# Weight sums of the four-quarter products formed on GpSimd, and the norms' scales loaded through ScalarE's queue

## Chip, core and metric

The kernel runs on one core of a Trainium2 chip. The metric is the device time of one execution in microseconds; lower is better. Three executions of the kernel before took 1226.11, 1226.34 and 1227.87 us.

## What is computed

The reference is one layer of a decoder trunk over 512 tokens of width 1024: a SwiGLU feed-forward network (FFN), a mixer (sparse attention, a short convolution and gates), attention over a memory, and a second FFN. Each stands between two RMS norms and is added to the running sum. The change lies in the two FFNs and in the load of the norms' scales:

```python
def rms_norm(x, g):
    xf = x.astype(jnp.float32)
    y = xf * lax.rsqrt(jnp.mean(xf * xf, axis=-1, keepdims=True) + EPS)
    return (y * g.astype(jnp.float32)).astype(x.dtype)
def swiglu(x, w1, w3, w2):
    return (jax.nn.silu(x @ w1) * (x @ w3)) @ w2
f = swiglu(rms_norm(h, ffn1_pre_g[l]), ffn1_w1[l], ffn1_w3[l], ffn1_w2[l])
h = h + 0.5 * rms_norm(f, ffn1_post_g[l])
```

The inner width of an FFN is 2816, that is 22 column blocks of 128.

## The kernel before

**Precision.** Every float32 operand of a product is split into a high part that TensorE takes (fp32r) and the remainder, and a product is three matmuls: high by high, high by low, low by high. `Weights.split` does it for weights: ScalarE casts the loaded tile `wraw` to `wh`, VectorE subtracts to `wl` (for a half tile both lie in one tile `whl`).

**Four-quarter products.** Most of the column blocks of `w1` and `w3` are not multiplied plainly. `ffn` takes two neighbouring blocks of one of the two matrices and `quad` forms their product with all 512 tokens by seven products of quarters instead of eight: the inner dimension of 1024 is cut in two, the two blocks are the other cut, and the tokens are cut in two halves. The text calls such a product a quad. There are 16 in FFN 1 and 18 in FFN 2; each pair of them (first `w1`, then `w3`) makes two blocks of the FFN's inner activations, and products with `w2` stand between. In `quad` each of the seven products is 12 matmuls of 128x256. They use, in this order, the weight factors "raw" (the upper block's two quarters, two products), "sums" (two products), "more" (two) and "last" (one). With the upper block's quarters T0, T1 and the lower block's L0, L1:

- sums: L0 + L1 and L0 + T0
- more: L0 + L1 + T0 and L0 + L1 + T0 + T1
- last: L1

**How the factors are made before.** `Weights.__init__` lists groups (one raw tile of 128x1024 each) and jobs (one split each). For a quad the group of sums loads L0 twice through SyncE's queue (SP), and `load` then issues two further transfers on GpSimd's queue (POOL) that add L1 and T0 to what lies in the tile while they move (`accum_op`, L126). When the job "sums" has been split, VectorE turns the same tile into "more" by two additions of 128x512 (L161, L162), and it is split again. The L1 quarters of a pair share one further tile. A pair takes five raw tiles.

**What sets the order.** `fetch` splits ahead of use, up to eight half tiles (`PIECES_AHEAD`), and each split calls `load` for the groups up to six tiles further (`RAW`, the raw tiles that there are). A scheduler then fixes the order of instructions on each engine when the program is built; each engine runs its own list in order, so an instruction that waits holds up all behind it. Loads signal through eight semaphores in turn, so a load on the hardware queues can be held until the load eight places earlier has landed. After the second quad of a pair VectorE multiplies the two results (`o<-o`), ScalarE casts the product (`hidh`, L321), and the weights of the next quads follow behind that cast in ScalarE's list.

**The start.** The scales of all norms (`gains`, 36 KB) are loaded once through POOL's queue (L293). ScalarE's queue carries two of the first weight tiles, SP's the rest and x. The first operand that TensorE needs is u = x times gain, made by `split_scaled` (L325 on ScalarE, then VectorE), and the first split weights `whl`.

Of the kernel before, what the change touches and what calls it, by code (L numbers as in the profile page):

```python
# [12 lines left out]
ALU = mybir.AluOpType  # L13
# [18 lines left out]
UNIT = 1024  # L32
PIECE = 512
# [40 lines left out]
class Weights:  # L74
# [6 lines left out]
    def __init__(self, tc, raw_pool, pool, items):  # L81
        self.nc, self.raw_pool, self.pool = tc.nc, raw_pool, pool
        self.items, self.groups, self.jobs, self.where = items, [], [], []
        room = 0
        for n, item in enumerate(items):
            src = item[0]
            if item[1] == "quad":
                self.where.append((len(self.jobs), 0))
                i, g = item[2], len(self.groups)
                top, low = src[0], src[1]  # L90
                self.groups.append([(top, 0, UNIT)])
                self.groups.append([(low[:, :PIECE], o, PIECE) for o in (0, PIECE)]
                                   + [(low[:, PIECE:], 0, 0), (top[:, :PIECE], PIECE, 0)])
                if i == 0:
                    last = g + 2
                    self.groups.append([(low[:, PIECE:], 0, PIECE), (item[3][1][:, PIECE:], PIECE, PIECE)])
                self.jobs += [(g, "raw", None), (g + 1, "sums", None), (g + 1, "more", None), (last, i, None)]
                room = 0
                continue
            w = src.shape[1]  # L100
            fresh = room < w
            if fresh:
                self.groups.append([])
                room = UNIT
            o = UNIT - room
            self.groups[-1].append((src, o, w))
            g = len(self.groups) - 1
            if n < FIRST:
                self.where.append((len(self.jobs), 0))
                self.jobs.append((g, o, o + w))  # L110
            elif fresh or o + w - self.jobs[-1][1] > UNIT:
                self.where.append((len(self.jobs), 0))
                self.jobs.append((g, o, o + w))
            else:
                self.where.append((len(self.jobs) - 1, o - self.jobs[-1][1]))
                self.jobs[-1] = (g, self.jobs[-1][1], o + w)
            room -= w
        self.raw, self.ready, self.held = {}, {}, {}
        self.nd = self.np = self.ni = 0

    def load(self, upto):
        while self.nd < min(upto, len(self.groups)):
            t = self.raw_pool.tile([P, UNIT], F32, tag="wraw", name="wraw", bufs=RAW)
            for src, o, w in self.groups[self.nd]:
                if w == 0:
                    self.nc.gpsimd.dma_start(t[:, o:o + PIECE], src, accum_op=ALU.add)  # L126
                    continue
                queue = self.nc.scalar if self.nd < 2 and o == 0 else self.nc.sync
                queue.dma_start(t[:, o:o + w], src)
            self.raw[self.nd] = t  # L130
            self.nd += 1

    def slots(self, j):
        _, c, end = self.jobs[j]
        return (2 if isinstance(c, str) else 1) if end is None else -(-(end - c) // PIECE)

    def split(self, src):
        shape = list(src.shape)
# [12 lines left out]
    def prepare(self, j):  # L151
        g, c, end = self.jobs[j]
        self.load(g + RAW)
        if end is not None:
            return self.split(self.raw[g][:, c:end])
        t = self.raw[g]
        if c in (0, 1):
            return self.split(t[:, c * PIECE:(c + 1) * PIECE])
        if c == "more":
            top, v = self.raw[g - 1], self.nc.vector  # L160
            v.tensor_add(t[:, :PIECE], t[:, :PIECE], top[:, :PIECE])  # L161
            v.tensor_add(t[:, PIECE:], t[:, :PIECE], top[:, PIECE:])  # L162
        return self.split(t.rearrange("p (j k) -> p j k", j=2))

    def ahead(self, upto):
        while self.np < min(upto, len(self.jobs)):
# [52 lines left out]
def build(tc, a, out):  # L219
    nc = tc.nc  # L220
    vec, ten = InOrder(tc, nc.vector), InOrder(tc, nc.tensor)
    ctx = ExitStack()
    with ctx:
# [36 lines left out]
        order = []  # L260
        for ffn in (1, 2):
            up, down = a[f"up{ffn}"], a[f"down{ffn}"]
# [16 lines left out]
            for p in ffn_plan(ffn):  # L279
                if p == ("plain", 0) or p == ("plain", 1):  # L280
                    order += [up[p[1], :, c] for c in (0, 1)] if ffn == 2 else []
                elif p[0] == "plain":
                    order += [up[p[1], :, c] for c in (0, 1)]
                elif p[0] == "quad":
                    order.append((up[p[1]:p[1] + 2, :, p[2]], "quad", p[2], up[p[1]:p[1] + 2, :, 1]))
                elif p[2][1] == 0:
                    order += across(p[2][0], p[1])
            order += across(0, len(SLABS) - 1) + across(1, len(SLABS) - 1)
# [1 line left out]


        gains = con.tile([P, len(GAINS), KD], F32, name="gains")
        nc.gpsimd.dma_start(gains, a["gains"])  # L293
        xts = [slot([P, 2, T], F32, "x") for _ in range(KD // 2)]
        x0 = [xts[i // 2][:, i % 2] for i in range(KD)]

# [608 lines left out]
        for c in range(4):  # L905
            pg, pc = bank("pgc"), bank("pci")
            product(pg, ws.unit(), u)
            t = ev([P, T], F32, "gc")
# [6 lines left out]
            for k in (1, 0):  # L915
                o = 2 - k
# [35 lines left out]
        for f in range(KD):  # L952
            if f < GATES:
                g = ga[f]
# [243 lines left out]
```

## Time and profile before

| | |
|---|---|
| median of three runs | 1226.34 us |
| the profiled execution's own time | 1225.09 us |
| its span, first to last instruction | 1223.3 us |
| TensorE (PE) busy | 1205.3 us, 99% |
| VectorE (DVE) busy | 861.1 us, 70% |
| ScalarE (ACT) busy | 569.4 us, 47% |
| GpSimd (POOL) busy | 82.9 us, 7% |
| bytes moved | 160.93 MB |

PE stands for matmuls and PEld for the weight loads before them, which overlap them. A row of the list of waits names who waited, at which line, for whom, and then the total in us, the number of waits and the longest one. In a timeline, the bracket at a row's end is the time that the engine had been idle and what ended it.

### The profile page before, as it was taken

The numbers are of one execution on the slowest core, as the hardware profiler recorded it, in microseconds if no ns is written. First come the engines' busy times: TensorE is split into PE (matmuls) and PEld (weight loads), VectorE is DVE, ScalarE is ACT, GpSimd is POOL, SyncE is SP. The second block draws the span as 40 slices with busy tenths as digits, with TensorE's granted clock in tenths as the row PEclk, the third lists the DMA queues.
The fourth block names the chain that finished last, engine by engine and source line by source line (L and its number), as shares of the span: only waits on it lengthen the run. The fifth ranks groups of instructions, "written<-read, shape, count | busy, mean of one in ns | idle before, by whom it ended". The sixth has DMA issues, their size and how long they took to land.

```text
span 1223.3 us, 18630 instructions
## 1 busy us (share of the span) xinstructions
PE 1205.3 (99%) x7198; PEld 1073.8 (88%) x7198; DVE 861.1 (70%) x1524; ACT 569.4 (47%) x991; POOL 82.9 (7%) x123
## 2 busy tenths in 40 slices
PE   7999999999999999999999999999999999999997
PEld 7889999999889888888887898888989999999986
DVE  6877577776777799964357785464768658776665
ACT  6445343433454365455453583453844434343241
POOL 0001111101002400000000000000000011110100
PEclk9999999999999999999999999999999999999999
DMA  8335656555715632222222545223435655755641
GB/s 311 86 93 155 163 142 173 157 155 137 242 60 155 174 120 84 77 90 79 69 70 86 172 121 172 69 77 131 139 68 155 155 144 155 176 156 142 145 139 69
DMA packets 62376, 160.93 MB, mean 132 GB/s; under 512 B 7872, under 2 KB 10432, under 8 KB 62288
## 3 DMA queue, kind: packets, MB, share of 16 engines
q1 hardware_dynamic: 50752, 138.74, 35.3%
q0 software_dynamic: 11104, 20.23, 10.0%
q8 instruction: 56, 0.92, 0.3%
q10 hardware_dynamic: 432, 0.79, 0.2%
q14 instruction: 32, 0.26, 0.1%
HBM read 150.81 MB, written 4.19 MB: 127 GB/s over the span
## 4 chain that ended last, share of the span: by engine, by line
PE 86%; DVE 7%; ACT 4%; issue 1%; DMA 1%; DVEq 0%; SPq 0%; ACTq 0%; POOLq 0%
PE q L212 28%; PE pf L212 21%; PE pgb L212 4%; PE ph L212 4%; PE pga L212 4%; PE pq L212 4%; PE pa L212 3%; PE pb L212 3%; PE pkx L212 2%; PE pvx L212 2%; ACT sq L432 2%; PE pya L212 2%; DVE f L212 2%; DVE wl L146 1%; PE pyb L212 1%
## 5 line engine op out<-in xcount | busy, mean ns | idle before, releaser
L146 DVE TENSOR_TENSOR wl<-wraw,wh 128x1024 fp32r<-128x1024 f32 x248 | 296.3, 1218 | 113.1 <-ACT wh L145 100.2
L145 ACT CAST wh<-wraw 128x1024 fp32r<-128x1024 f32 x248 | 253.2, 1049 | 112.0 <-DVE wraw L162 91.7
L212 PE MATMUL q<-rt,wh 128*128 128x256 f32 x816 | 148.4, 283 | 0.0
L212 PEld LDWEIGHTS q<-rt,wh 128*128 128x128 f32 x816 | 127.3, 192 | 0.0
L126 POOL DMA_DIRECT2D wraw<-in_up x68 | 58.6, 924 | 947.3 <-DMA wraw<-in_up 705.4
L212 PE MATMUL q<-rt,wl 128*128 128x256 f32 x408 | 115.7, 283 | 0.0
L212 PE MATMUL pf<-wh,hidh 128*128 128x512 f32 (+1 forms) x278 | 107.3, 386 | 0.0
L212 PE MATMUL pf<-wl,hidh 128*128 128x512 f32 (+1 forms) x278 | 107.2, 385 | 0.0
L212 PE MATMUL pf<-wh,hidl 128*128 128x512 f32 (+1 forms) x278 | 106.9, 384 | 0.0
L212 DVE TENSOR_TENSOR o<-o,q 128x512 f32<-128x512 f32 (+1 forms) x136 | 71.8, 549 | 12.0 <-PE q L212 9.7
L212 PE MATMUL q<-u,wh 128*128 128x256 f32 x432 | 79.2, 283 | 0.0
L212 PEld LDWEIGHTS q<-rt,wl 128*128 128x128 f32 x408 | 78.3, 192 | 0.3 <-DVE wl L146 0.3
L212 PE MATMUL q<-r,wh 128*128 128x256 f32 x384 | 70.4, 283 | 0.0
L212 PEld LDWEIGHTS q<-u,wh 128*128 128x128 f32 x432 | 68.4, 192 | 1.3
L212 PEld LDWEIGHTS q<-r,wh 128*128 128x128 f32 x384 | 60.9, 192 | 1.2
L212 PEld LDWEIGHTS pf<-wh,hidl 128*128 128x128 f32 x278 | 52.3, 188 | 10.5
L212 PE MATMUL q<-u,wl 128*128 128x256 f32 x216 | 61.1, 283 | 0.0
L212 PEld LDWEIGHTS pf<-wh,hidh 128*128 128x128 f32 x278 | 52.3, 188 | 9.8
L212 PEld LDWEIGHTS pf<-wl,hidh 128*128 128x128 f32 x278 | 52.3, 188 | 9.5
L321 ACT CAST hidh<-o 128x1024 fp32r<-128x1024 f32 x17 | 17.9, 1052 | 91.9 <-DVE o L212 91.9
L212 PE MATMUL pgb<-u,wh 128*128 128x512 f32 x192 | 59.3, 389 | 0.0
L212 DVE TENSOR_TENSOR f<-f,pf 128x512 f32<-128x512 f32 (+1 forms) x49 | 33.0, 673 | 33.0 <-PE pf L212 32.7
(265 smaller groups left out, 2671.6 us busy)
## 6 DMA issues: line engine op xcount, KB each, us to landing
wraw<-in_up SPq DMA_DIRECT2D x108, 256.0 KB, 4.7
wraw<-in_up SPq DMA_DIRECT2D x50, 512.0 KB, 5.2
wraw<-in_down SPq DMA_DIRECT2D x44, 512.0 KB, 4.4
wraw<-in_w_in SPq DMA_DIRECT2D x37, 512.0 KB, 4.5
wraw<-in_up POOLq DMA_DIRECT2D x68, 256.0 KB, 5.5
wraw<-in_w_out SPq DMA_DIRECT2D x8, 512.0 KB, 3.7
wraw<-in_w_k SPq DMA_DIRECT2D x8, 512.0 KB, 4.1
wraw<-in_w_v SPq DMA_DIRECT2D x8, 512.0 KB, 4.5
```

The costliest lines, as they stand in the source:

```text
L126: self.nc.gpsimd.dma_start(t[:, o:o + PIECE], src, accum_op=ALU.add)
L145: self.nc.scalar.copy(hi, src)
L146: self.nc.vector.tensor_sub(lo, src, f32(hi))
L212: ins = f(*args, **kwargs)
L321: nc.scalar.copy(dst_h, src)
L432: ins = nc.scalar.activation(ev([P, T], F32, "sq")[:, cols], src, AF.Square, accum_out=part)
```

## The change

Each quad now has three raw tiles. Two are loaded, the upper block and the lower block, each once and whole (512 KB). The third is not loaded: two GpSimd additions fill it with "sums" (L123, L124 of the new file), and when that has been split, two more GpSimd additions turn it into "more" (L157, L158). "last" is read from the lower block's tile. The two loads of L0, the shared L1 loads, the two accumulating transfers and VectorE's two additions are gone. The load of `gains` moves from POOL's queue to ScalarE's, ahead of the two weight loads there. Lines after the edit move up by some four, so that the subtraction of `split` is L146 before and L141 now.

```diff
-                i, g = item[2], len(self.groups)
-                top, low = src[0], src[1]
-                self.groups.append([(top, 0, UNIT)])
-                self.groups.append([(low[:, :PIECE], o, PIECE) for o in (0, PIECE)]
-                                   + [(low[:, PIECE:], 0, 0), (top[:, :PIECE], PIECE, 0)])
-                if i == 0:
-                    last = g + 2
-                    self.groups.append([(low[:, PIECE:], 0, PIECE), (item[3][1][:, PIECE:], PIECE, PIECE)])
-                self.jobs += [(g, "raw", None), (g + 1, "sums", None), (g + 1, "more", None), (last, i, None)]
+                g = len(self.groups)
+                self.groups += [[(src[0], 0, UNIT)], [(src[1], 0, UNIT)], []]
+                self.jobs += [(g, "raw", None), (g + 2, "sums", None), (g + 2, "more", None), (g + 1, "last", None)]
...
             for src, o, w in self.groups[self.nd]:
-                if w == 0:
-                    self.nc.gpsimd.dma_start(t[:, o:o + PIECE], src, accum_op=ALU.add)
-                    continue
                 queue = self.nc.scalar if self.nd < 2 and o == 0 else self.nc.sync
                 queue.dma_start(t[:, o:o + w], src)
+            if not self.groups[self.nd]:
+                top, low = self.raw[self.nd - 2], self.raw[self.nd - 1]
+                self.nc.gpsimd.tensor_add(t[:, :PIECE], low[:, :PIECE], low[:, PIECE:])
+                self.nc.gpsimd.tensor_add(t[:, PIECE:], low[:, :PIECE], top[:, :PIECE])
...
-        if c in (0, 1):
-            return self.split(t[:, c * PIECE:(c + 1) * PIECE])
-        if c == "more":
-            top, v = self.raw[g - 1], self.nc.vector
-            v.tensor_add(t[:, :PIECE], t[:, :PIECE], top[:, :PIECE])
-            v.tensor_add(t[:, PIECE:], t[:, :PIECE], top[:, PIECE:])
-        return self.split(t.rearrange("p (j k) -> p j k", j=2))
+        if c == "last":
+            return self.split(t[:, PIECE:])
+        res = self.split(t.rearrange("p (j k) -> p j k", j=2))
+        if c == "sums":
+            top, add = self.raw[g - 2], self.nc.gpsimd.tensor_add
+            add(t[:, :PIECE], t[:, :PIECE], top[:, :PIECE])
+            add(t[:, PIECE:], t[:, :PIECE], top[:, PIECE:])
+        return res
...
-        nc.gpsimd.dma_start(gains, a["gains"])
+        nc.scalar.dma_start(gains, a["gains"])
```

The order in which the built program's instructions stand moves at three places that the prediction speaks of.

ScalarE at the start of the program; DMAHW0 to DMAHW7 are the eight semaphores of the hardware queues, DMASW0 is that of POOL's queue. Before:

```order
L129 DMA wraw<-in_up 128x512 x2
L307 ACT_TABLE_LOAD
L307 ACTIVATE warm<-ones 128x1 [waits DVE_49]
L349 ACTIVATE sq<-x 128x256 [waits DMAHW1_49]
L325 ACTIVATE u<-x,gains 128x256 [waits DMASW0_49]
L145 CAST whl<-wraw 128x512 [waits DMAHW0_49]
```

Now:

```order
L289 DMA gains<-in_gains 128x72
L120 DMA wraw<-in_up 128x512 x2
L303 ACT_TABLE_LOAD
L303 ACTIVATE warm<-ones 128x1 [waits DVE_49]
L345 ACTIVATE sq<-x 128x256 [waits DMAHW1_49]
L321 ACTIVATE u<-x,gains 128x256 [waits DMAHW0_49]
L140 CAST whl<-wraw 128x512 [waits DMAHW2_49]
```

The scales are now the first issue of this queue and the first of the eight semaphores is theirs; the two weight loads come one issue later.

SyncE's queue at the start. Before:

```order
L298 DMA x<-in_x 128x2x256
L129 DMA wraw<-in_up 128x512
L298 DMA x<-in_x 128x2x256
L129 DMA wraw<-in_up 128x512
L298 DMA x<-in_x 128x2x256 x2
L129 DMA wraw<-in_up 128x512 [waits DMAHW0_49]
```

Now:

```order
L294 DMA x<-in_x 128x2x256
L120 DMA wraw<-in_up 128x512
L294 DMA x<-in_x 128x2x256
L120 DMA wraw<-in_up 128x512
L294 DMA x<-in_x 128x2x256
L294 DMA x<-in_x 128x2x256 [waits DMAHW0_49]
```

The fourth load of x, which waited for nothing, now waits until the scales have landed.

VectorE in FFN 1, from the low part of the activations that the quads 13 and 14 made (`hidl`) to the splits of the quad 15, whose raw tiles are 2762 and 2795 before. Before:

```order
L212 TENSOR_TENSOR hidl_3046<-o_2921,hidh_3045 128x1024
L212 TENSOR_TENSOR f_1031<-f_1031,pf_3067 128x512
L146 TENSOR_TENSOR wl_3053<-wraw_2795,wh_3052 128x1024
L161 TENSOR_TENSOR wraw_2795<-wraw_2795,wraw_2762 128x512
L162 TENSOR_TENSOR wraw_2795<-wraw_2795,wraw_2762 128x512
L146 TENSOR_TENSOR wl_3059<-wraw_2795,wh_3058 128x1024
L146 TENSOR_TENSOR whl_3064<-wraw_2923,whl_3064 128x512
```

VectorE now, at the same place (sums of quad 15 are 2899, its lower block 2774):

```order
L208 TENSOR_TENSOR hidl_3020<-o_2897,hidh_3019 128x1024
L208 TENSOR_TENSOR f_1025<-f_1025,pf_3041 128x512
L141 TENSOR_TENSOR wl_3029<-wraw_2899,wh_3028 128x1024
L141 TENSOR_TENSOR wl_3035<-wraw_2899,wh_3034 128x1024
L141 TENSOR_TENSOR whl_3038<-wraw_2774,whl_3038 128x512
```

GpSimd now, for the quads 15 (its sums are 2899, its blocks 2772 and 2774) and 16 (sums 2999, blocks 2933 and 2964):

```order
L123 TENSOR_TENSOR wraw_2899<-wraw_2774 128x512
L124 TENSOR_TENSOR wraw_2899<-wraw_2774,wraw_2772 128x512
L123 TENSOR_TENSOR wraw_2999<-wraw_2964 128x512
L124 TENSOR_TENSOR wraw_2999<-wraw_2964,wraw_2933 128x512
L157 TENSOR_TENSOR wraw_2899<-wraw_2899,wraw_2772 128x512
L158 TENSOR_TENSOR wraw_2899<-wraw_2899,wraw_2772 128x512
```

GpSimd had no arithmetic there before. VectorE's two additions are gone, and the split of "more" comes right behind that of "sums" in its list; GpSimd has the same two additions behind the sums of the next quad.

## Rows read from the trace of the kernel before

**Rows 1.** The page: the span, and busy time of the engines.

```profile
span 1223.3 us, 18630 instructions
PE 1205.3 (99%) x7198; PEld 1073.8 (88%) x7198; DVE 861.1 (70%) x1524; ACT 569.4 (47%) x991; POOL 82.9 (7%) x123
```

**Rows 2.** Waits of PE, whole span: the two longest of four.

```profile
PE ph L212 <- ACT whl L145: 8.1, 1, 8.1
PE po L212 <- ACT pth L321: 0.7, 3, 0.3
```

**Rows 3.** Chain that ended last, first 60 us: start us, us, what.

```profile
1.28 5.72 DMA gains<-in_gains
7.02 0.51 ACT u L325
...
8.09 21.81 PE ph L212 x165
```

**Rows 4.** Timelines of ACT and SP, start: start us, us, what.

```profile
0.74 0.98 ACTq L129 DMA_DIRECT2D wraw<-in_up  x2
5.48 0.42 ACT L349 ACTIVATE sq<-x 128x256 f32<-128x256 f32 x1 [2.24 <-DMA x<-in_x]
10.70 1.71 ACT L325 ACTIVATE u<-x,gains 128x256 fp32r<-128x256 f32 x4
...
2.73 1.21 SPq L298 DMA_DIRECT2D x<-in_x  x2
```

**Rows 5.** DMA issues of short stretches at the start, and one of the mixer: us to landing.

```profile
wraw<-in_up ACTq DMA_DIRECT2D x1, 256.0 KB, 4.5
x<-in_x SPq DMA_DIRECT2D x1, 256.0 KB, 4.7
x<-in_x SPq DMA_DIRECT2D x2, 256.0 KB, 6.5
...
qa<-rh SPq DMA_DIRECT2D x8, 64.0 KB, 2.0
```

**Rows 6.** Groups of instructions, whole span: count, busy us and mean ns.

```profile
L161 DVE TENSOR_TENSOR wraw<-wraw 128x512 f32<-128x512 f32 x34 | 23.4, 689 | 0.8
L811 POOL TENSOR_SCALAR_AFFINE_SELECT bias<-bias 128x256 f32<-128x256 f32 x2 | 0.8, 409 | 0.0
L811 POOL TENSOR_SCALAR_AFFINE_SELECT bias<-bias 128x512 f32<-128x512 f32 x1 | 0.6, 613 | 0.1
```

**Rows 7.** Timelines of DVE, ACT and PEld around quad 15; last row, quad 33.

```profile
291.81 1.23 DVE L212 TENSOR_TENSOR o<-o 128x1024 f32<-128x1024 f32 x1
295.97 1.22 DVE L146 TENSOR_TENSOR wl<-wraw,wh 128x1024 fp32r<-128x1024 f32 x1
297.22 0.69 DVE L161 TENSOR_TENSOR wraw<-wraw 128x512 f32<-128x512 f32 x1
297.94 0.69 DVE L162 TENSOR_TENSOR wraw<-wraw 128x512 f32<-128x512 f32 x1
299.83 1.23 DVE L146 TENSOR_TENSOR wl<-wraw,wh 128x1024 fp32r<-128x1024 f32 x1 [1.19 <-ACT wh L145]
...
298.75 1.05 ACT L145 CAST wh<-wraw 128x1024 fp32r<-128x1024 f32 x1 [3.60 <-DVE wraw L162]
...
301.11 0.19 PEld L212 LDWEIGHTS q<-rt,wl 128*128 128x128 f32 x1 [0.17 <-DVE wl L146]
...
1156.10 0.19 PEld L212 LDWEIGHTS q<-rt,wl 128*128 128x128 f32 x1 [0.17 <-DVE wl L146]
```

**Rows 8.** Timelines of DVE and PEld: "more" of quad 9.

```profile
207.77 1.22 DVE L146 TENSOR_TENSOR wl<-wraw,wh 128x1024 fp32r<-128x1024 f32 x1
...
211.71 0.19 PEld L212 LDWEIGHTS q<-rt,wl 128*128 128x128 f32 x1
```

**Rows 9.** Stretches: busy us of PE, PEld, DVE, ACT and POOL, clock, DMA share.

```profile
198.60:228.60 30.00, 30.00 (x230) 29.02 (x229) 24.73 (x34) 11.16 (x14) 1.73 (x2) 1.00 0.59 161
1060.00:1090.00 30.00, 30.00 (x216) 28.39 (x215) 24.31 (x33) 13.35 (x16) 3.44 (x4) 1.00 0.49 129
```

More of the change, by code (lines that the diff above doesn't have):

```diff
@@ L134, in slots @@
         _, c, end = self.jobs[j]
-        return (2 if isinstance(c, str) else 1) if end is None else -(-(end - c) // PIECE)
+        return (1 if c == "last" else 2) if end is None else -(-(end - c) // PIECE)
     def split(self, src):
@@ L284, in build @@
                 elif p[0] == "quad":
-                    order.append((up[p[1]:p[1] + 2, :, p[2]], "quad", p[2], up[p[1]:p[1] + 2, :, 1]))
+                    order.append((up[p[1]:p[1] + 2, :, p[2]], "quad"))
                 elif p[2][1] == 0:
```

## The prediction

> **What bounds the kernel now.** Read the busy times first, then who waits, then the two places where something waits.
>
> TensorE is busy for 1205.3 of 1223.3 us [rows 1]. The list of waits shows why the rest is small: its longest wait is 8.1 us at the very start, the next kind comes to 0.7 us in all [rows 2]. So the work that the change takes from VectorE (70% busy) and from the DMA queues is work that TensorE hardly ever waits for. A faster VectorE is worth nothing by itself; what counts is the start, and any place where a weight factor is ready just in time.
>
> The start is in the chain of waits: the scales are issued at 1.28 us and land 5.72 us later, ScalarE's u follows at 7.02 and the first matmul at 8.09 [rows 3]. In ScalarE's timeline x was there at 5.48, where its square begins; u then waits for the scales alone [rows 4].
>
> For the quads, take for each split the time at which VectorE's subtraction ends and the time at which TensorE first loads the result. Quad 15 is the tightest: the subtraction for "more" begins at 299.83 and takes 1.23, and TensorE, idle for 0.17 us, loads that factor at 301.11. Quad 33, in FFN 2, is its twin with the same 0.17 [rows 7]. The next ones are quad 9 and its twin: the subtraction ends at 207.77 + 1.22 = 208.99, the load is at 211.71, so the lead is 2.7 us [rows 8]. In the remaining 30 quads the smallest lead of a factor of sums or "more" is larger than that. Quad 15 is tight because its sums are split behind the cast of the activations in ScalarE's list, and "more" can only follow.
>
> **The start, part by part.** The scales now go out as the first issue of ScalarE's queue, at about 0.74 instead of 1.28. The two weight loads there move by one issue, 0.98 / 2 = 0.49 us [rows 4]; the first landed after 4.5 us, so at 5.24, now about 5.73. If the scales are in by then, u follows the square, at 5.48 + 0.42 = 5.90 instead of 7.02, and the weights are there for the cast behind it. The first matmul keeps its distance of 8.09 - 7.02 = 1.07 and begins at 6.97: **-1.1 us**. Do the scales land in time? 36 KB on a hardware queue may take 2.0 us as the mixer's 64 KB transfers do, or 4.7 us as the first 256 KB of x did [rows 5]. That gives 2.7 or 5.4 us. I take the short end, since the size is nearest to it.
>
> The same load has a second effect. The fourth load of x used to go out right behind the third (2.73 and about 3.3 us) and now waits for the scales. It took 6.5 us [rows 5] and is read by the third of the four u's from 10.70 on, at about 11.5, or 10.4 if all moves by 1.1. With the scales in at 2.7 to 3.3 nothing changes (3.3 + 6.5 = 9.8). With 5.4 it lands at 11.9, 1.5 us late, and the gain is lost. So the term lies between -1.2 (the square's own wait shortened a little) and 0; I take **-1.1**.
>
> **VectorE's additions, 68 of 689 ns** [rows 6], 46.8 us off an engine that TensorE does not wait for: 0 everywhere but in the tight quads. Work that hides them: the matmuls themselves, ahead of which the splits run.
>
> **GpSimd's additions, 136 of 128x512.** No row shows a two-input operation there. One bound from below is VectorE's own 0.69. From above: GpSimd's one-input select of 128x512 takes 0.613 us, and 0.613 - 0.409 = 0.204 us per 256 columns, so reading both inputs in turn costs 2 x 0.613 = 1.23, or, paying the fixed part once, 1.02 [rows 6]. I take 1.15, between these two, since they are rows of the same engine. By the Trainium skill (GPSIMD Engine Reference, section 3.1, a two-input add of 2048 columns in 4497 ns) an estimate for 512 is 1.1 to 1.2; the sum would be the same.
>
> In quad 15 the chain is now: subtraction for the sums ends at 295.97 + 1.22 = 297.19; hand-over 0.1; two additions, 2.3; hand-over 0.1; cast at 299.7. Before, the cast began at 298.75 [rows 7]. So "more" is 0.95 us late and TensorE already waits there: **+0.95**, and the same in quad 33: **+1.9** together. The bounds: additions at 0.69 give 0; at 1.23, +1.1 each. In the other 32 quads 0.95 us fits in the lead of 2.7 us or more; were that lead gone, each would cost up to the same.
>
> **Loads.** Per quad 1.75 MB of reads becomes 1 MB, and two stages, the load and the accumulating load behind it, become one load and two additions. Cost 0, hidden by splits that run a quad ahead. Against that a pair of quads holds six raw tiles instead of five, all there are, so a lower block's load waits until the quad two places earlier has split its "last". The shorter way from load to sums pays for this; I count 0. GpSimd's transfers for the mixer's queries and keys stand behind the last addition of FFN 1 in its list and before the first of FFN 2; they meet none of them: 0.
>
> **Sum.** -1.1 + 1.9 = +0.8 on the profiled execution's 1225.09 us. The median of the three runs, 1226.34, lies 1.25 above that execution, so I expect **1227.1 us**. A measurement of this kernel can tell about 0.2%, 2.5 us, from no change; this forecast lies inside.
>
> **Rivals.**
>
> *The additions and VectorE hold each other up (slower).* The mechanism would be one door to the memory that both use: a GpSimd addition holds up a VectorE operation with both inputs in SBUF, for its whole length. The splits, the product of a pair (`o<-o`, 1.23 us) and its low part are of that kind; operations that read a PSUM bank are not. Price: in the stretch 198.6 to 228.6 VectorE is busy for 24.73 us, of which six additions, 4.1 us, go; three quads bring 12 x 1.15 = 13.8, and 34.4 us do not fit in 30 [rows 9]. 4.4 us over, less the lead of 2.7 in quad 9, is +1.7; the twin stretch, 24.31 us, gives +1.3. In quads 15 and 33 one operation of the tight chain would wait up to 1.15 more for the sums of the next quad, which stand ahead in GpSimd's list: +2.3. With the sum above: +0.8 + 5.3 = +6.1, **1232.4 us**. It decides when an addition takes more than (30 - 20.6) / 12 = 0.78 us and truly excludes VectorE. Against it: much of VectorE's time reads PSUM, it has pauses that additions can use, such as the 1.19 us before the split of "more" [rows 7], and only a lateness beyond the lead reaches TensorE. The Trainium skill (SBUF — State Buffer, section "Who interferes with whom") speaks for it: it gives VectorE and GpSimd one shared pair of ports, locked for a whole instruction, and names a two-input VectorE operation against a GpSimd operation that reads. No run here shows it: GpSimd has only selects and fills, and those stand beside no two-input work. Chance 0.25.
>
> *The scales come late (no gain at the start).* On the hardware queue they land at 5.4, the fourth x is late, and only the +1.9 stays: 1228.2 us. The rows for 36 KB speak against it, the slow landings of everything at the start for it. Chance 0.12.
>
> *The tight quads hold (only the start shows).* GpSimd's additions run at VectorE's speed, or the sums of quad 15 come earlier since their load is one stage shorter: -1.1, 1225.2 us. Against it: the split of the sums stands behind the activations' cast in ScalarE's list before and now, so an earlier load does not help. Chance 0.13. The rest, **0.50**, is the forecast.
>
> **How the numbers follow.** The forecast's own range, from additions at 1.0 to 1.4 us and a start of -1.1 to -0.6, is 1226.5 to 1228.6. The range to name reaches down to the third rival with the whole gain at the start (-1.2, 1225.1, and half a microsecond for the runs' own spread): 1224.6; and up to the first rival: 1232.6. Slower by over 0.2% (above 1228.8) is most of the first rival, a third of the second and a tenth of the forecast: 0.21 + 0.04 + 0.05 = 0.30. Faster (below 1223.9) needs something at the start that I don't see: 0.07. The rest, 0.63, is no change that can be told.
>
> **What would show it.** In the profile after: the chain's first wait no longer names the scales, and the first matmul begins near 7.0 us (right) or near 8 (second rival). GpSimd shows 136 additions; their mean, 1.15 or not, prices the tight quads. TensorE's weight loads wait for `wl` once in each FFN for about 1.1 us, in quads 15 and 33 (right), not at all (third rival), or in many quads, with VectorE's splits longer than 1.22 us or held behind GpSimd (first rival). VectorE's busy time falls by about 47 us, and bytes moved by some 27 MB, 34 quads by 0.75 MiB. The prediction is wrong if TensorE's waits in the quads come to more than 4 us, or if the raw tiles run short, which would show as casts that wait for loads.

## The result and the profile after

The changed kernel takes 1240.83 us in the median (four runs, 1240.11 to 1242.55), the kernel before beside it 1226.53 us. The ratio is 1.0117, with a 95% interval from 1.0099 to 1.0134. Forecast were 1227.1 us and a range up to 1232.6: **wrong, by 13.7 us, and 8.2 above the range's end**.

The page's spans and busy times, the answer to [rows 1]:

```profile
span 1240.7 us, 18440 instructions
PE 1212.0 (98%) x7198; PEld 1077.7 (87%) x7198; DVE 840.0 (68%) x1456; ACT 566.5 (46%) x991; POOL 215.3 (17%) x190
```

VectorE was to lose 46.8 us and lost 21.1: something stretches what is left. Bytes moved fall from 160.93 to 134.17 MB, as counted. TensorE's busy time grows by 6.7 us for the same 7198 matmuls, so part of that work ran slower or stood under waits (below).

TensorE's waits, the answer to [rows 2] (who waited, line, for whom; total us, times, longest):

```profile
PE ph L208 <- ACT whl L140: 6.5, 1, 6.5
PE q L208 <- DVE o L208: 5.3, 3, 2.5
PE ph L208 <- DVE u L208: 3.1, 2, 2.3
PE psc L208 <- issue: 1.6, 1, 1.6
PE q L208 <- DVE wl L141: 1.5, 2, 0.8
PE pf L208 <- DVE wl L141: 0.7, 1, 0.7
```

The start is shorter (6.5 against 8.1), but there are waits now that were not there. The largest, `q <- DVE o`, is no wait for a weight factor. `o` is what VectorE reads out of a bank of PSUM, and the next product of the quad needs that bank.

TensorE's matmuls are the same in both programs, so their start times can be set one against the other. The lag (after minus before) moves as follows:

| where | lag gained, us |
|---|---|
| first matmul -1.58, by 13 us still | -0.81 |
| quad 8 | +0.67 |
| quad 13 | +4.07 |
| quad 15 | +1.22 |
| mixer, product of queries and keys (`psc`) | +1.70 |
| start of FFN 2 (`ph`, at 880 before) | +2.21 |
| a product with `w2` at 944 before | +1.01 |
| six steps of 0.2 to 0.4 (at 254, 376, 958, 1034, 1048 and 1109 before), together | +1.55 |
| quad 31, the twin of 13 | +4.27 |
| quad 33, the twin of 15 | +1.22 |

The sum is +17.1; at the last matmul the lag is 17.2 us, and the spans differ by 17.4. The medians differ by 14.3; the two profiled executions are not each at its kernel's median, so the table overstates by some 3 us in all.

**Quad 13.** GpSimd's, ScalarE's and VectorE's timelines, then TensorE's (start us, us; in brackets the idle time before and what ended it):

```profile
258.47 1.29 POOL L123 TENSOR_TENSOR wraw<-wraw 128x512 f32<-128x512 f32 x1 [6.48 <-DMA wraw<-in_up]
259.72 1.28 POOL L124 TENSOR_TENSOR wraw<-wraw 128x512 f32<-128x512 f32 x1
260.96 1.29 POOL L157 TENSOR_TENSOR wraw<-wraw 128x512 f32<-128x512 f32 x1
262.32 1.29 POOL L158 TENSOR_TENSOR wraw<-wraw 128x512 f32<-128x512 f32 x1
...
263.65 1.05 ACT L140 CAST wh<-wraw 128x1024 fp32r<-128x1024 f32 x1 [6.94 <-POOL wraw L158]
...
264.73 1.23 DVE L141 TENSOR_TENSOR wl<-wraw,wh 128x1024 fp32r<-128x1024 f32 x1 [6.24 <-ACT wh L140]
265.87 0.68 DVE L208 TENSOR_TENSOR o<-o,q 128x512 f32<-128x512 f32 x1
...
266.60 0.50 PE L208 MATMUL q<-r,wh 128*128 128x256 f32 x2 [2.34 <-DVE o L208]
```

Read it from below. TensorE waits for the bank that `o<-o,q` frees. That operation stands behind the split of "more" in VectorE's list, which waits for ScalarE's cast, which waits for GpSimd's L158. L157 and L158, the additions for quad 13's "more", stand in GpSimd's list behind L123 and L124, the sums of quad **14**, and those wait 6.48 us for their load. All four additions take 1.29 us here, and the split its usual 1.23: nothing is stretched. It is a chain of lists in order, begun by a late load.

The load is late because a raw tile came free late. The load that ended the 6.48 us is the second of quad 14, 4.0 us on its way. It goes out when the split of quad 12's "more" has ended, which came behind quad 12's L158 (GpSimd's, VectorE's and SP's timelines):

```profile
250.70 1.29 POOL L158 TENSOR_TENSOR wraw<-wraw 128x512 f32<-128x512 f32 x1
...
253.11 1.23 DVE L141 TENSOR_TENSOR wl<-wraw,wh 128x1024 fp32r<-128x1024 f32 x1 [5.06 <-ACT wh L140]
...
254.36 0.33 SPq L120 DMA_DIRECT2D wraw<-in_up  x1
```

The waits of GpSimd, ScalarE and SP on one another in the whole run:

```profile
SPq L120 <- POOL wraw L158: 209.7, 34, 12.6
...
POOL wraw L123 <- DMA wraw<-in_up: 109.7, 19, 8.9
...
ACT wh L140 <- POOL wraw L158: 183.6, 32, 10.5
```

SP's loads wait 34 times, once a quad, for L158, the last reader of an upper block's tile, which they are to fill, and the loads after them stand behind in SP's queue; the sums wait for their load; the cast waits for L158 again. It is a ring: a late "more" makes the loads two quads on late, and with them the next "more".

After the stall the matmuls run slower for a while. Stretches of TensorE's time (us, busy us and count of PE, of PEld, of DVE, of ACT, of POOL, granted clock, DMA share, GB/s):

```profile
264.00:266.00 2.00, 0.27 (x3) 0.06 (x1) 1.27 (x2) 1.21 (x2) 0.00 (x0) 1.00 0.69 158
266.00:268.00 2.00, 1.40 (x9) 1.40 (x10) 1.97 (x5) 0.00 (x0) 0.00 (x0) 0.85 0.53 162
268.00:270.00 2.00, 2.00 (x12) 2.00 (x11) 1.86 (x3) 0.00 (x0) 0.00 (x0) 0.50 0.85 320
270.00:272.00 2.00, 2.00 (x15) 2.00 (x15) 0.83 (x2) 1.59 (x2) 0.00 (x0) 0.79 0.37 147
```

The granted clock falls from 1.00 to 0.50 of 2.4 GHz, that is to 1.2 GHz, after TensorE has stood idle for 2.3 us, and is back by 272; 0.85 and 0.79 are means of stretches that hold both levels. Of the 4.1 us in quad 13, 2.7 come at the stall and the first matmuls behind it, 1.4 from the slower matmuls after. Quad 31 does the same (idle for 2.53 us, then means of 0.60 and 0.55 in two stretches).

**The start of FFN 2** is something else. GpSimd's and VectorE's timelines there, of after:

```profile
883.48 1.29 POOL L123 TENSOR_TENSOR wraw<-wraw 128x512 f32<-128x512 f32 x1 [447.15 <-DVE wl L141]
884.73 2.27 POOL L124 TENSOR_TENSOR wraw<-wraw 128x512 f32<-128x512 f32 x1
...
882.18 7.04 DVE L141 TENSOR_TENSOR wl<-wraw,wh 128x1024 fp32r<-128x1024 f32 x4
889.14 1.25 DVE L208 SCALAR_TENSOR_TENSOR u<-pu,gains,u 128x256 fp32r<-128x256 f32 x3
```

and VectorE's of before:

```profile
874.86 4.81 DVE L146 TENSOR_TENSOR wl<-wraw,wh 128x1024 fp32r<-128x1024 f32 x4
```

Four splits that took 4.81 us take 7.04 beside the first two additions, and one addition takes 2.27 instead of 1.29. TensorE waits 2.3 us for the `u` behind them. VectorE and GpSimd do hold each other up. This idle time is as long as that of quad 13, yet here the clock stays up, so the step is 2.2 us and no more:

```profile
888.00:890.00 2.00, 0.33 (x2) 0.33 (x3) 2.00 (x5) 0.35 (x1) 0.00 (x0) 1.00 0.64 178
```

GpSimd's groups, the price that [rows 6] could only bound (busy us, mean ns, idle us before them and its releasers):

```profile
L124 POOL TENSOR_TENSOR wraw<-wraw 128x512 f32<-128x512 f32 x34 | 53.7, 1580 | 0.0
L123 POOL TENSOR_TENSOR wraw<-wraw 128x512 f32<-128x512 f32 x34 | 51.3, 1509 | 659.1 <-DVE wl L141 498.1 <-DMA wraw<-in_up 109.7 <-DVE o L208 36.3
L157 POOL TENSOR_TENSOR wraw<-wraw 128x512 f32<-128x512 f32 x34 | 44.7, 1314 | 200.9 <-DVE wl L141 200.9
L158 POOL TENSOR_TENSOR wraw<-wraw 128x512 f32<-128x512 f32 x34 | 44.1, 1298 | 2.3
```

Alone an addition takes 1.29 us, above all of my rows; the sums' additions, often beside VectorE, take 1.5 to 1.6 in the mean.

### The profile page after: what moved, and what is told of

Its sections match the earlier page's. It is cut to its first block, busy times and chain, and to the rows that moved or that the text cites. A ratio compares the mean times of both kernels' runs of the same rounds, so it can differ in the third digit from the quotient of the medians.

```text
span 1240.7 us, 18440 instructions
## 1 busy us (share of the span) xinstructions
PE 1212.0 (98%) x7198; PEld 1077.7 (87%) x7198; DVE 840.0 (68%) x1456; ACT 566.5 (46%) x991; POOL 215.3 (17%) x190
## 2 busy tenths in 40 slices
DMA packets 42902, 134.17 MB, mean 108 GB/s; under 512 B 5824, under 2 KB 8384, under 8 KB 42816
## 4 chain that ended last, share of the span: by engine, by line
PE 61%; DVE 17%; ACT 7%; POOL 6%; issue 4%; DMA 3%; DVEq 0%; ACTq 0%; SPq 0%; POOLq 0%
PE pf L208 14%; PE q L208 11%; DVE wl L141 6%; PE pgb L208 4%; PE ph L208 4%; DVE o L208 4%; PE pga L208 4%; PE pq L208 4%; PE pa L208 3%; PE pb L208 3%; DMA wraw<-in_up 3%; ACT wh L140 2%; POOL wraw L158 2%; POOL wraw L157 2%; PE pkx L208 2%
## 5 line engine op out<-in xcount | busy, mean ns | idle before, releaser
L141 DVE TENSOR_TENSOR wl<-wraw,wh 128x1024 fp32r<-128x1024 f32 x248 | 309.1, 1271 | 167.8 <-ACT wh L140 165.3
L123 POOL TENSOR_TENSOR wraw<-wraw 128x512 f32<-128x512 f32 x34 | 51.3, 1509 | 659.1 <-DVE wl L141 498.1
L157 POOL TENSOR_TENSOR wraw<-wraw 128x512 f32<-128x512 f32 x34 | 44.7, 1314 | 200.9 <-DVE wl L141 200.9
```

Of the source, the lines that this page charges most:

```text
L123: self.nc.gpsimd.tensor_add(t[:, :PIECE], low[:, :PIECE], low[:, PIECE:])
L141: self.nc.vector.tensor_sub(lo, src, f32(hi))
```

## The experiments

Three theories. **Theory 1:** the order of GpSimd's list, "more" behind the next quad's sums, sets the time. **Theory 2:** VectorE and GpSimd hold each other up, my first rival. **Theory 3:** six raw tiles are too few for three a quad. All ratios are to the kernel before, run beside.

### The scales alone

```diff
-        nc.gpsimd.dma_start(gains, a["gains"])
+        nc.scalar.dma_start(gains, a["gains"])
```

> The kernel before with only the load of the scales moved to ScalarE's queue. All theories agree on the quads here (nothing of them is changed): no waits beyond those of before. If the start of the changed kernel (first matmul 1.58 us earlier, 1.16 us by 11.7 us) comes from this edit, the time is 1.2 us under the kernel before, ratio 0.9990, and the first matmul begins near 6.5. If the scales' load in the changed kernel also caused the 1.9 us lost at the mixer (its place among the eight load semaphores), the gain is gone: ratio 1.0005.

Measured: 1225.13 us, ratio 0.9986, interval 0.9977 to 0.9995. ScalarE's timeline at the start of this kernel, the answer to [rows 4]:

```profile
0.74 0.44 ACTq L293 DMA_DIRECT2D gains<-in_gains  x1
...
4.08 0.42 ACT L349 ACTIVATE sq<-x 128x256 f32<-128x256 f32 x1 [0.41 <-DMA x<-in_x]
4.41 0.49 ACT L325 ACTIVATE u<-x,gains 128x256 fp32r<-128x256 f32 x1
5.66 0.62 ACT L145 CAST whl<-wraw 128x512 fp32r<-128x512 f32 x1 [0.76 <-DMA wraw<-in_up]
...
7.96 0.51 ACT L325 ACTIVATE u<-x,gains 128x256 fp32r<-128x256 f32 x1 [0.76 <-DMA x<-in_x]
```

The scales land 2.6 us after their issue, u no longer waits for them, and the first matmul is 1.76 us earlier. A later tile of x is what the third u waits for (7.96), and by 13 us 0.28 us is left in the trace. By the medians this part of the change is a gain of 1.8 us. The traces don't show where: the profiled execution (1225.22) is at its kernel's median, that of the kernel before (1225.09) below its own. It is the only kernel of this study that is faster than the one before.

### All additions on VectorE

```diff
-                self.nc.gpsimd.tensor_add(t[:, :PIECE], low[:, :PIECE], low[:, PIECE:])
-                self.nc.gpsimd.tensor_add(t[:, PIECE:], low[:, :PIECE], top[:, :PIECE])
+                self.nc.vector.tensor_add(t[:, :PIECE], low[:, :PIECE], low[:, PIECE:])
+                self.nc.vector.tensor_add(t[:, PIECE:], low[:, :PIECE], top[:, :PIECE])
...
-            top, add = self.raw[g - 2], self.nc.gpsimd.tensor_add
+            top, add = self.raw[g - 2], self.nc.vector.tensor_add
```

> The changed kernel with all four additions on VectorE in place of GpSimd; loads, tiles and the scales as changed. Theory 1 (GpSimd's list: the additions for more stand behind the next quad's sums, which wait for their load): the additions keep their dependences but lose GpSimd's 1.29 us each and its list; the 2.8 and 2.95 us stalls in quads 13 and 31 go, 1226 to 1229 us, ratio 1.000 to 1.002. Theory 2 (VectorE and GpSimd hold each other up): nothing is left to hold VectorE up, its 0.69 us additions cost 94 us of its idle time, 1225 to 1227. Theory 3 (three raw tiles a quad out of six come free too late): the sums still wait for the same loads, now in VectorE's list, where they hold up the bank evacuations as well: 1238 or more, ratio above 1.009.

Measured: 1227.70 us, ratio 1.0007 (0.9998 to 1.0016). With nothing on GpSimd the same loads and tiles bring no loss against the kernel before. Against the scales alone (1225.13, run beside) they cost 2.6 us: in the trace TensorE loses 1.4 us at the start of FFN 2, where the sums now stand in VectorE's own list, and nothing in the quads. Theory 3 by itself, which gave 1238 or more, falls; 1 and 2 both stand.

### The sums issued later, and a seventh raw tile

```diff
-            if not self.groups[self.nd]:
-                top, low = self.raw[self.nd - 2], self.raw[self.nd - 1]
-                self.nc.gpsimd.tensor_add(t[:, :PIECE], low[:, :PIECE], low[:, PIECE:])
-                self.nc.gpsimd.tensor_add(t[:, PIECE:], low[:, :PIECE], top[:, :PIECE])
...
+        if c == "raw":
+            s, low, add = self.raw[g + 2], self.raw[g + 1], self.nc.gpsimd.tensor_add
+            add(s[:, :PIECE], low[:, :PIECE], low[:, PIECE:])
+            add(s[:, PIECE:], low[:, :PIECE], t[:, :PIECE])
+            return self.split(t.rearrange("p (j k) -> p j k", j=2))
```

> The changed kernel with the two additions for the sums issued at the split of the same quad's raw factor, not at its load, so that GpSimd's list reads sums, more, sums, more, quad after quad. Theory 1 (list order): the 4.2 and 4.4 us lost in quads 13 and 31 go, and part of quads 8, 15 and 33: 1229 to 1232 us, ratio 1.003 to 1.005. Theory 2 (contention): the same 136 additions stand beside the same VectorE work, 1238 to 1242. Theory 3 (ring): loads wait as before, 1238 to 1242.

Measured: 1233.35 us, ratio 1.0054 (1.0041 to 1.0067). The other kernel of this pair:

```diff
-SLOTS, RAW, EV, ACC = 43, 6, 10, 6
+SLOTS, RAW, EV, ACC = 42, 7, 10, 6
```

> The changed kernel with seven raw tiles instead of six, and 42 slots instead of 43 for the split factors to pay for the space. Theory 1 (list order): the next quad's sums wait less, since their load starts earlier, but still stand ahead of more: half of the 8.6 us of quads 13 and 31 goes, 1234 to 1238. Theory 2 (contention): 1239 to 1242. Theory 3 (ring): the load of a lower block no longer waits for a tile, and nearly all of the loss in the quads goes: 1228 to 1232, ratio 1.002 to 1.005.

Measured: 1231.87 us, ratio 1.0044 (1.0031 to 1.0056). TensorE's waits, first of the kernel with the later sums:

```profile
PE q L209 <- DVE o L209: 2.0, 2, 1.0
PE q L209 <- DVE wl L137: 1.5, 2, 0.8
```

then of the kernel with seven tiles:

```profile
PE psc L208 <- issue: 1.8, 1, 1.8
PE q L208 <- DVE wl L141: 1.5, 2, 0.8
PE ps_rows L208 <- DVE y L208: 1.5, 1, 1.5
```

With the later sums the wait for `o` falls from 5.3 to 2.0 us, the lag in each of quads 13 and 31 to 1.2 us, with 0.7 just ahead of each, so the time lies 1.4 us above theory 1's range. With seven tiles that lag is gone, and so are the steps in quad 8, at 944 and at 1034 to 1048; the time is in theory 3's range and below theory 1's. Either cut, of the list or of the ring, takes out most of the same loss: 1 and 3 are two links of one chain. GpSimd does the same 136 additions in both, and VectorE's splits of whole tiles are stretched no less (313.6 and 312.6 us in all, 308.4 in the changed kernel), so theory 2 doesn't explain that loss. Of the lag in quads, seven tiles leave one step of 1.2 us in quad 15 and one in quad 33, near the +0.95 each that I had forecast. Besides these, that trace loses 1.6 us in the norm at 30 us, 1.0 in the norm at 861, and 3.5 from `psc` on, 1.6 of them at a lower clock after 1.8 us without a matmul.

### "More" on VectorE alone, the sums on VectorE alone

```diff
-            top, add = self.raw[g - 2], self.nc.gpsimd.tensor_add
+            top, add = self.raw[g - 2], self.nc.vector.tensor_add
```

> The changed kernel with the two additions for more on VectorE, as before the change, and only the sums on GpSimd, six raw tiles. Theory 1 (list order: more stands behind the next quad's sums in GpSimd's list): more no longer stands in that list, the stalls of quads 13 and 31 go, and the chain of quads 15 and 33 is the old one with two 0.69 us additions: 1225 to 1228 us, ratio 0.999 to 1.001. Theory 2 (VectorE and GpSimd hold each other up): half of GpSimd's additions stay, so half of the loss: 1231 to 1234. Theory 3 (six raw tiles are too few): the upper block's tile is given back two additions of 0.69 instead of 1.29 us after the split, about 1.2 us sooner, of 4 to 9 us that the sums wait: 1235 or more.

Measured: 1230.30 us, ratio 1.0032 (1.0019 to 1.0044). In the quads only 0.27 us is left, at quad 33; the largest step of the lag is now 3.6 us at the start of FFN 2, 2.2 at the stall and 1.4 behind it, where the granted clock is 0.56 and 0.59 in the mean of two stretches of 2 us. So moving "more" out of the list breaks the chain too, though above the time that theory 1 gave and below theory 2's: the two engines' hold on each other at FFN 2's start was in neither theory's account of the quads.

```diff
-                self.nc.gpsimd.tensor_add(t[:, :PIECE], low[:, :PIECE], low[:, PIECE:])
-                self.nc.gpsimd.tensor_add(t[:, PIECE:], low[:, :PIECE], top[:, :PIECE])
+                self.nc.vector.tensor_add(t[:, :PIECE], low[:, :PIECE], low[:, PIECE:])
+                self.nc.vector.tensor_add(t[:, PIECE:], low[:, :PIECE], top[:, :PIECE])
```

> The other half: the sums' additions on VectorE, the two for more on GpSimd. Theory 1 (list order): GpSimd's list holds nothing that waits for loads, so the stalls of quads 13 and 31 go; the chain of quads 15 and 33 keeps two 1.29 us additions: 1.2 us each, as measured with seven raw tiles (1.17): 1228 to 1231 us, ratio 1.001 to 1.004. Theory 2 (contention): half of the loss, 1231 to 1234. Theory 3 (ring): sums wait for their loads in VectorE's list now: 1236 or more.

Measured: 1236.47 us, ratio 1.0085 (1.0072 to 1.0099), which no theory gave but the third by its threshold. The wait of 2.8 us in quads 13 and 31 is gone, as theory 1 has it, but quads 15 and 33 now lose 2.0 and 5.3 us, and in FFN 2 there are steps of 0.9 to 1.4 us in four other places. Of the 5.3 us, 1.4 come at a lower granted clock (0.59 and 0.56 in the mean from 1168 to 1172), which quad 15 doesn't have. VectorE's list holds 28 waits of the sums for loads, 33.3 us in all (12.8 with all additions on VectorE). A slow "more" on GpSimd and sums that hold up VectorE seem to add up; this was not taken apart further.

### The two tight quads

```diff
-            top, add = self.raw[g - 2], self.nc.gpsimd.tensor_add
+            tight = [[i for i, job in enumerate(self.jobs) if job[1] == "sums"][n] for n in (14, 32)]
+            top, add = self.raw[g - 2], (self.nc.vector if j in tight else self.nc.gpsimd).tensor_add
```

> The kernel with seven raw tiles, and in quads 15 and 33 alone the two additions for more on VectorE. If the two tight quads lose their time to the length of GpSimd's additions (2 x 1.29 against 2 x 0.69 us), the +1.17 us that TensorE loses in each goes: 2.3 us under the kernel with seven tiles, 1229 to 1230 us. If they lose it because the sums of those quads come later, or because VectorE is held up there, nothing changes: 1231 to 1232.5.

Measured: 1229.26 us, ratio 1.0023 (1.0014 to 1.0032), 2.6 us less for 2 x 1.2. TensorE's lag has no step in any quad now, with 132 additions still on GpSimd. So the length of the additions was what those two quads lost by. What is left stands elsewhere; GpSimd's and VectorE's timelines of this kernel, in the norm ahead of FFN 2:

```profile
854.59 1.28 POOL L123 TENSOR_TENSOR wraw<-wraw 128x512 f32<-128x512 f32 x1 [424.51 <-DVE stat L209]
855.83 1.29 POOL L124 TENSOR_TENSOR wraw<-wraw 128x512 f32<-128x512 f32 x1
...
854.46 0.16 DVE L209 TENSOR_TENSOR stat<-stat 128x1 f32<-128x1 f32 x1
854.66 2.47 DVE L209 SCALAR_TENSOR_TENSOR stat<-stat 128x1 f32<-128x1 f32 x2
```

Two operations of one column, 0.35 us together before the change, take 2.47: they end when the second addition does. `pu`, the next product, starts after 2.0 us without a matmul, and the products behind it run slower (granted clock 0.50 from 866 to 868): 3.6 us of lag in this norm, 0.6 of which FFN 2's start gives back. At 30.69 `c<-c,v`, two columns, takes 1.20 us instead of 0.16 beside another addition, for about 1 us of lag.

### Contention by itself

The next kernel makes all sums on VectorE and lets GpSimd do 136 additions that nobody needs:

```diff
...
+        if c in ("sums", "more"):
+            for _ in range(2):
+                self.nc.gpsimd.tensor_add(self.spare, f32(res[0][1]), f32(res[1][1]))
...
+        ws.spare = con.tile([P, PIECE], F32, name="spare")
```

> The kernel with all additions on VectorE (1227.7 us), and besides 136 additions of 128x512 on GpSimd, four a quad, that read the remainders just split and write a tile that nobody reads; nobody waits for them. 42 slots instead of 43 pay for that tile. It measures contention alone. Theory 2 as I priced it (an addition shuts VectorE's operations with both inputs in SBUF out for its whole length, four a quad): VectorE now has 94 us more of such work than in the changed kernel, so at least the 5.3 us of that rival, 1233 us or more. Theory 1 or 3 (contention hardly reaches TensorE): within 1.5 us of the kernel without them, 1227 to 1229.

Measured: 1262.02 us, ratio 1.0290 (1.0275 to 1.0304). The control for the slot:

```diff
-SLOTS, RAW, EV, ACC = 43, 6, 10, 6
+SLOTS, RAW, EV, ACC = 42, 6, 10, 6
```

> The kernel with all additions on VectorE (1227.7 us), with 42 slots instead of 43 and nothing else: the control of the two kernels with idle work and of those with seven raw tiles. All theories: 1227 to 1229 us. If a missing slot is what costs, 1232 or more, and the idle additions are worth that much less.

Measured: 1227.51 us, ratio 1.0010 (1.0002 to 1.0019). And copies of one input in place of the additions:

```diff
-            for _ in range(2):
-                self.nc.gpsimd.tensor_add(self.spare, f32(res[0][1]), f32(res[1][1]))
+            for _ in range(4):
+                self.nc.gpsimd.tensor_copy(self.spare, f32(res[0][1]))
```

> As the kernel with the 136 idle additions (1262.0 us), but each pair of additions becomes four copies of 128x512, one input each, started by the same split; nobody waits for them. By the selects on GpSimd a one-input pass takes 0.613 us, so they fill about the same time. If what GpSimd and VectorE share is held for the length of a GpSimd instruction that reads, whatever it computes: each hold is half as long, the sum about the same, 1245 to 1262 us. If only the two-input additions hold it: 1227 to 1230.

Measured: 1229.69 us, ratio 1.0029 (1.0019 to 1.0038). Against the control the additions cost 34.5 us, the copies 2.2. By its time alone the kernel with the copies falls where it was expected if only two-input additions hold VectorE up; the durations say otherwise. The groups of GpSimd's idle work and of one of VectorE's additions for "more" (L161), first beside the additions:

```profile
L157 POOL TENSOR_TENSOR spare<-wl 128x512 f32<-128x512 f32 x136 | 218.4, 1606 | 873.5 <-DVE wl L141 868.2
...
L161 DVE TENSOR_TENSOR wraw<-wraw 128x512 f32<-128x512 f32 x34 | 42.9, 1262 | 0.6
```

then beside the copies:

```profile
L157 POOL COPY spare<-wl 128x512 f32<-128x512 f32 x272 | 258.3, 950 | 802.4 <-DVE wl L141 788.5
...
L161 DVE TENSOR_TENSOR wraw<-wraw 128x512 f32<-128x512 f32 x34 | 29.3, 863 | 0.6
```

GpSimd is busy for longer with the copies, yet VectorE's splits and additions gain 34 us by them and 83 by the additions (sums of these groups, less those of the kernel with all additions on VectorE). A copy adds at most 0.42 us to a 0.68 us addition of VectorE (the longest take 1.10), an addition 1.1 (1.78): no more than GpSimd's instruction lasts. Both hold; the long hold is the dear one. The loss does not follow the sum in proportion. That the extra 34 us mostly fit in leads such as those of [rows 7, 8] and the 83 do not is my reading, not shown; a part of the 34.5 us is slower matmuls (mean granted clock 0.991, in the control 0.998). These idle additions start the moment a split ends, when VectorE begins its next operation, so they meet it more often than those of the changed kernel do. The 34.5 us are no measure of contention there.

### The first sums off the norms

The kernel with seven tiles and two tight quads on VectorE, and the sums of the first quad of FFN 1 and the first two of FFN 2 issued later:

```diff
-            if not self.groups[self.nd]:
+            first = [j[0] for j in self.jobs if j[1] == "sums"]
+            if not self.groups[self.nd] and self.nd not in (first[0], first[16], first[17]):
...
+        if c == "raw" and [j[0] for j in self.jobs if j[1] == "sums"].index(g + 2) in (0, 16, 17):
+            res = self.split(t.rearrange("p (j k) -> p j k", j=2))
+            s, low, add = self.raw[g + 2], self.raw[g + 1], self.nc.gpsimd.tensor_add
+            add(s[:, :PIECE], low[:, :PIECE], low[:, PIECE:])
+            add(s[:, PIECE:], low[:, :PIECE], t[:, :PIECE])
+            return res
```

> The kernel with seven raw tiles and two tight quads on VectorE (1229.26 us), and the sums of the first quad of FFN 1 and of the first two of FFN 2 issued at the split of their own raw factor instead of at their load. Theory 2, in a new place (GpSimd's additions of the first quads fall beside the norms ahead of the FFNs, whose 128x1 and 128x2 operations on VectorE are on the path: 2.47 us for two of them at 854.66 instead of 0.35): the additions move off the norms, the 1.0 us at 32 us and the 2 to 3.6 us at 861 us go, 1225 to 1227 us. If those gaps have another cause: 1229 to 1230. Between these, if the additions now meet the first splits instead.

Measured: 1226.46 us, ratio 1.0002 (0.9993 to 1.0011). TensorE's waits, and then VectorE's group of splits:

```profile
PE ph L216 <- ACT whl L141: 7.2, 1, 7.2
PE po L216 <- ACT pth L325: 0.7, 3, 0.3
PE ph L216 <- DVE u L216: 0.7, 1, 0.7
PE ps_stat L216 <- DVE rows L216: 0.7, 2, 0.4
```

```profile
L142 DVE TENSOR_TENSOR wl<-wraw,wh 128x1024 fp32r<-128x1024 f32 x247 | 315.5, 1299 | 149.5 <-ACT wh L141 136.6 <-PE q L216 8.6 <-ACT p L870 3.3
```

Three cuts (a tile, two quads, three pairs of additions moved) bring the time back to that of the kernel before, with 132 of 136 additions still on GpSimd. The scales alone had given 0.9986, so by the medians some 1.7 us of the loss may be left; the profiled execution is the fastest of eleven and doesn't show them. The splits of this group take 315.5 us against 295.8 with no additions on GpSimd. In the quads VectorE is held up by some 20 us in all, and TensorE sees none of it.

## Why the prediction was wrong

**The start** was right in kind; its size was in part luck. I had -1.1 by scales that land in time, u behind the square and a first matmul at 6.97. The scales land 2.5 us after their issue, and the first matmul begins at 6.51. x landed sooner than in [rows 4] (the square begins at 4.01 instead of 5.48), so u is early, and what the first matmul waits for is now the first weight load, in at 5.82, near the 5.73 that I had for it. By 13 us -0.81 is left. In the other kernels with the scales on ScalarE's queue it is anything from -1.23 to +0.76 in one trace each, though they start alike. That rival, scales that come late, falls. The second effect that I named, a fourth load of x held up by the scales, does not show: the four u's that need it run without a pause from 9.62. What shows is one that I had not named: the third u waits for the second load of x, 0.4 us here and 0.8 with the scales alone.

**The tight quads** were right in kind: quads 15 and 33, by the length of the two additions. +0.95 each became 1.2, in the changed kernel and with seven tiles, since an addition takes 1.29 us and not 1.15; worked with 1.29, the chain gives 1.22. Both bounds that I built from GpSimd's one-input rows, 1.02 and 1.23, were too low. The rival that these quads hold falls with it.

**The step that failed is "Loads": "The shorter way from load to sums pays for this; I count 0."** I had named that a pair holds six tiles of six, and had a lower block's load wait for the split of "last". I had not joined to it that an upper block's tile is free only after the last addition for "more", L158, which now is on the engine that also waits for loads; and the lower block's load of quad 14 went out at 254.36, when the split of "more" ended, which waits for L158 as well. I read GpSimd's list only for what its transfers meet and not for what stands ahead of "more". The sign that I gave for tiles that run short, casts that wait for loads, named the wrong engine: GpSimd's sums wait for them, 109.7 us in all, and ScalarE's casts 1.2. The order of the list, the sums of quad 14 ahead of "more" of quad 13, is fixed before any run; with the wait of the sums for their load it makes a ring. That is where quads 13 and 31 lose 8.3 of the 17.2 us, a part of that as slower matmuls after the stall; that a stall can cost again by the clock behind it, 1.4 to 1.5 us in each, was in no term of mine.

**A second step failed with it: "in the other 32 quads 0.95 us fits in the lead of 2.7 us or more".** I measured leads from the split to TensorE's first load of that factor. The stall was not there. A split that comes late holds up what stands behind it in VectorE's list, the read-out of a bank, and that had no lead in my account.

**My first rival** had the mechanism and the wrong place. VectorE and GpSimd do hold each other up, for up to the length of an instruction: the idle additions show it alone. By the Trainium skill (SBUF — State Buffer, section "Who interferes with whom") a VectorE instruction with two inputs in SBUF contends with a GpSimd instruction that reads; the runs agree, for copies as well as additions, and for operations of one column. I priced it by adding up busy times in a stretch (4.4 us over, 1.7 us lost in quad 9). That sum found nothing: in the quads some 20 us of holding-up cost nothing once the ring was cut. It costs where VectorE's small operations are themselves the path, in the norms, and where the first splits stand ahead of `u`: 2.2 us at FFN 2's start in the changed kernel, 1.0 and 3.6 us in two norms of the kernel with seven tiles and two quads on VectorE. At FFN 2's start the sums on VectorE cost 1.1 to 1.4 us as well, with nothing beside them, so not all of the 2.2 is the hold.

**Still open:** the 1.70 us at `psc` in the mixer. With seven tiles it is 1.96, in the others 1.1 or less, and almost nothing with all additions on VectorE and 43 slots, with "more" there, or in the last kernel. In the two worst VectorE waits longest for the load of the cosines (2.6 and 2.9 us against 1.7), but with the scales alone it waits 2.4 and loses 0.3. No run was made for it. Of quad 33 with the sums on VectorE, the stall ahead of the slower matmuls is as open.

## What to carry to other kernels

When work moves to an engine that was idle, write out that engine's new list with the waits in it, and follow each item behind a waiting one to whoever needs it, buffers that it gives back included: a tile freed by the last link can close a ring through a load. Measure slack at everything that stands behind a late instruction on its engine, not only at the consumer of its result. And GpSimd work beside VectorE is cheap next to bulk operations with slack, dear next to a chain of small ones.

## What the runs showed that I had not expected

- A one-column operation of VectorE with its inputs in SBUF waits out GpSimd's additions: 2.47 us for two that take 0.35.
- A two-input addition of 128x512 on GpSimd takes 1.29 us undisturbed, a copy as little as 0.614; a copy held a 0.68 us addition of VectorE up by at most 0.42 us, an addition by 1.1.
- After 2.3 and 2.5 us without a matmul, in the middle of a kernel that otherwise runs at a granted clock of 1.00, the clock fell to 0.50 and cost another 1.4 to 1.5 us each time. It is no fixed price of a stall: 2.34 us at FFN 2's start left the clock at 1.00 in the changed kernel and brought it down with "more" on VectorE. Of that kernel's five executions the one with a mean granted clock of 0.999 took 1229.00 us, the four with 0.997 took 1229.75 to 1231.12.
- 36 KB through ScalarE's queue landed in 2.5 us in the changed kernel, through GpSimd's in 5.7 in the kernel before, each at the start beside the loads of x and the weights.
